# The row copy of each tile's softmax sums is held in the zone of nine buffers, not in the zone of four

## The chip, the cores and the metric

The kernel runs on one core of a Trainium2 chip. The metric is the device time of one execution in microseconds; smaller is better. A core has five engines that run their own instruction streams in order: TensorE (PE in the profile; its weight loads are listed as PEld), VectorE (DVE), ScalarE (ACT), GpSimd (POOL) and the sync engine, whose stream here only issues DMA transfers (SPq). They wait for each other through semaphores. Data lies in on-chip memory, in accumulators that TensorE writes (banks), and in the chip's main memory.

## The reference

One step of a model with two layers on 1024 latent tokens and 256 context tokens, 1024 channels wide. Layer 0 projects the normalised and modulated input to queries, keys, values and gates of two attention mixers: A attends to all keys, B to a window of 128 tokens on each side, with a learned extra logit ("sink") in the softmax; both see all context keys. The outputs are multiplied by SiLU gates and projected back. Layer 1 mixes with a Fourier transform over positions and channels, gated, and projected. A final normalisation follows.

What matters for this change is the softmax's denominator. Cut to the lines that compute it:

```python
def softmax_sink(sc, sink):
    sink = sink.astype(jnp.float32)
    m = jnp.maximum(jnp.max(sc, axis=-1, keepdims=True), sink)
    p = jnp.exp(sc - m)
    return p / (jnp.sum(p, axis=-1, keepdims=True) + jnp.exp(sink - m))
...
return jnp.concatenate([oa * jax.nn.silu(ga), ob * jax.nn.silu(gb)], axis=-1) @ w_out
```

The kernel doesn't divide the probabilities. It sums them, takes reciprocals once for each tile of 128 tokens and all 16 heads, and multiplies these into the gate before the output projection.

## The kernel before, in words

**Tiles and units.** The 1280 tokens are ten tiles `t` of 128 rows (0 to 7 latent, 8 and 9 context). Attention runs in units `(t, g, pr)`: `g` = 0, 1 are the two key/value heads of mixer A, 2 and 3 those of mixer B, and `pr` a pair of heads. A unit has two halves. `soft` (lines 941 to 1018) computes scores on TensorE, running minima on VectorE (lines 967, 1011) and the exponential on ScalarE (line 974), which also leaves the sum of each head in `SU`. `weigh` (line 1040) transposes the probabilities on TensorE (line 1050), splits them into a high and a low part (ScalarE through the helper at line 277, VectorE at line 1053), and multiplies them with the values (line 1056). Then ScalarE copies the lower half of the accumulator into a buffer `lo_sb` (line 1065), VectorE adds it to the upper half in a buffer `os_` (line 1067), and a store of `os_` to `od` in main memory is kept in `held` until the next unit (line 1073).

`attend` walks through the units of mixer A, then those of mixer B in the order 0 2 3 4 7 6 5 1 8 9 of the tiles; in mixer B `weigh` runs two units behind `soft`. Between the units a `Filler` puts in other work: gates (`gate0`: a tanh buffer `th` at line 822, the gate `gs` at line 826, stored to `gd` at lines 838 to 844), loads and splits of the output weights (`out_weights`, load at line 1112, splits in lines 277 and 283), folding of a weight for layer 1 (`fold_piece`), and output projections of tiles that are complete (`proj_in`, `proj_step`, `out_proj`).

**The row copy.** When the last unit of a tile in mixer B is done, `after` calls `totals(t)`. It adds the sink terms, sums, takes reciprocals on VectorE (lines 1023 to 1029), transposes the 128 x 16 result to 16 x 128 on TensorE (line 1032), copies it from the accumulator into a buffer `row` on ScalarE (line 1035) and stores it to `scd` in main memory (line 1037: one or two pieces, as the tiles are stored in another order of tokens). `proj_in` reads `scd` back, spread over the partitions (line 1225), and GpSimd multiplies it with the gate and that with `od` (lines 1226 and 1227).

**Zones.** On-chip buffers lie in zones. `ZONES` gives the number of buffers and their width in words of 4 bytes: "h" has 9 of 512 words (2 KB in each partition), "e" has 4 of 256 words (1 KB).

```python
ZONES = {"u": (26, 1032), "w": (8, 1032), "q": (2, 1024), "pt": (3, 1024), "p": (4, 1280), "h": (9, 512), "e": (4, 256)}
```

`take(tag, shape)` takes the buffer of a zone that was dropped longest ago, and `drop` puts one at the end of the zone's queue. Both happen when the program is written down, in the order of the code, so which buffer follows which is fixed and doesn't depend on times. An instruction that writes a taken buffer waits until all users of the buffer's earlier content are done: readers on an engine, or a store that must have landed.

In this stretch "e" serves `lo_sb`, `os_` and, before the change, `row`. "h" serves `th` and `gs` of the gates, the raw halves of weight rows before they are split (line 1112), pieces of the fold, and scratch of the projections (`yt` in lines 1247 and 1347).

**Order.** The order of the instructions on each engine is not that of the code. The program is made with `schedule_with_timeline_sim=True`: a planner goes through all instructions with due times of its own model, and lets each engine issue what is ready first, with the dependences through the buffers as given. So when the buffer of an instruction changes, its dependences change, and the planned order can change from there on. On the chip each engine then follows this fixed order, and one that waits holds up all that stands behind it. Only for the first phase is the order on the sync engine written out by hand; it ends before the stretch that the change touches.

Of the kernel before, what the change touches and what calls it, by code (L numbers as in the profile page):

```python
# [17 lines left out]
P = 128  # L18
# [121 lines left out]
def hybrid_step(ctx: ExitStack, tc: tile.TileContext, I, O):  # L140
# [15 lines left out]
    def take(tag, shape, dt=F32):  # L156
        tags = (tag,) if isinstance(tag, str) else tag
        z = min((t for t in tags if spare[t]), key=lambda t: spare[t][0])
        i = spare[z].popleft()[1]
        size = 2 if dt == BF16 else 4  # L160
        for s in shape[1:]:
            size *= s
        assert size <= 4 * ZONES[z][1]
        made[0] += 1
        return Buf(z, i, up.tile(list(shape), dt, tag=f"{z}{i}", name=f"{z}{made[0]}", bufs=1))

    def drop(*bufs):
        for b in bufs:
            stamp[0] += 1
            spare[b.zone].append((stamp[0], b.idx))  # L170
# [5 lines left out]
    def t_bank(name, dt=F32):  # L176
        return bank("t", name, dt)
# [843 lines left out]
    def totals(t):  # L1021
        tot = sm.tile([P, 16], F32, tag="tot", name=f"tot{t}", bufs=2)
        dve.tensor_add(tot[:, 0:8], NM[:, t], sink)  # L1023
        act.activation(SU[:, t, 8:16, 1], tot[:, 0:8], AF.Exp)
        dve.tensor_reduce(out=tot, in_=SU[:, t], op=ALU.add, axis=AX.X)
        dve.tensor_scalar(tot, tot, 2.0, None, op0=ALU.mult)
        dve.reciprocal(tot, tot)
        byp = sm.tile([P, 16], F32, tag="byp", name=f"byp{t}", bufs=2)
        dve.tensor_copy(byp.rearrange("p (h c) -> p h c", h=2), tot.rearrange("p (c h) -> p h c", h=2))  # L1029
        tot = byp  # L1030
        tp = t_bank(f"tt{t}")
        pe.transpose(tp[0:16, 0:P], tot, ident)
        row = take("e", (16, P))
        rev = t in (2, 3, 6, 7, 9)
        act.activation(row[..., ::-1] if rev else row.a, tp[0:16, 0:P], AF.Copy)
        for r, c0, b0, n in PIECES[t]:
            sp.dma_start(scd[r, :, :, c0 : c0 + n].rearrange("h c n -> (h c) n"), row[:, b0 : b0 + n])
        drop(row)
# [158 lines left out]
    def after(un):  # L1197
        t, g, pr = un
        if g > 1:
            clock[0] += 1  # L1200
        if g < 2 and un == lastA[g]:
            swap_kv(g)
        if un == last_g2:
            drop(*kvb[2])
        if g == 3 and pr == 1:
            totals(t)
            finished[t] = clock[0]
# [772 lines left out]
```

## Time and profile before

| | |
|---|---|
| median of 3 runs | 1191.29 us (1189.96 to 1192.39) |
| the profiled execution's own time | 1188.89 us |
| its span, first to last instruction | 1187.1 us |
| TensorE busy, share of the span | 1150.7 us, 97% |
| VectorE, ScalarE, GpSimd busy | 835.5, 569.4, 329.3 us |
| mean granted TensorE clock | 0.998 |
| row copies (line 1035) | 10, first at 596.7 us, last at 803.0 us |
| stores of rows (line 1037) | 16, first at 599.4 us |

How to read it: times are microseconds from the start of the span. In a list of groups or a timeline a line gives start, duration, engine, line of the kernel, operation, what is written and read (buffer numbers left out, and a zone's name stands for its buffers), and in brackets how long the engine stood idle before it and what ended that. In a table by stretches there stand for each engine its busy time and its number of instructions, then the granted clock as a share of full speed, the share in which the DMA engines were busy, and GB/s. The chain of waits is followed back from the last instruction, at each step to what released it.

### The profile page before, as it was taken

What the parts mean: (1) busy time and instruction counts of PE and PEld (TensorE: products, weight loads), DVE (VectorE), ACT (ScalarE), POOL (GpSimd) and SP (SyncE); (2) the same over time, 40 slices, a digit from 0 to 9 for tenths busy, and PEclk for the clock granted to TensorE, in tenths of its full rate; (3) what the DMA queues carried; (4) which work ended last, traced back from release to release, by engine and by line L of the source; (5) the groups of instructions that cost most, each with busy time, mean ns of one, the idle gap of its engine ahead of it and who ended that gap; (6) DMA issues with size and microseconds to landing.
All of it is one profiled execution on the core that took longest, in us unless ns stands there. A gap on an engine that the chain in (4) does not pass through costs nothing.

```text
span 1187.1 us, 22024 instructions
## 1 busy us (share of the span) xinstructions
PE 1150.7 (97%) x8103; PEld 1032.0 (87%) x8103; DVE 835.5 (70%) x1994; ACT 569.4 (48%) x1149; POOL 329.3 (28%) x294
## 2 busy tenths in 40 slices
PE   8999999999999999999999989999999999999997
PEld 6788899999999999899989887887877888998886
DVE  2489788877777776668888977876765962378543
ACT  4442455556656555556666674522363234342211
POOL 2355645512222221010110045275331226100001
PEclk9999999999999999999999999999999999999999
DMA  9978512323523232344352586785213426264321
GB/s 330 374 252 265 172 44 67 103 78 105 161 72 96 77 96 76 87 126 123 86 153 75 149 233 201 226 256 160 89 45 129 165 93 189 95 205 152 125 107 54
DMA packets 130096, 168.81 MB, mean 142 GB/s; under 512 B 26298, under 2 KB 86454, under 8 KB 129988
## 3 DMA queue, kind: packets, MB, share of 16 engines
q1 hardware_dynamic: 127476, 158.74, 43.4%
q0 software_dynamic: 2368, 8.39, 2.4%
q8 instruction: 64, 1.05, 0.4%
q14 instruction: 44, 0.36, 0.1%
q10 hardware_dynamic: 144, 0.26, 0.1%
HBM read 123.19 MB, written 44.16 MB: 141 GB/s over the span
## 4 chain that ended last, share of the span: by engine, by line
PE 76%; DMA 10%; DVE 6%; ACT 3%; issue 2%; SPq 2%; POOL 1%; POOLq 0%; DVEq 0%; ACTq 0%
PE of L265 9%; PE av L1056 9%; PE ga L265 8%; PE pt L1050 8%; PE q L265 8%; PE sL L933 5%; PE oz L265 4%; PE u L265 4%; PE g1O L265 4%; PE g1E L265 3%; PE kv L265 3%; PE sC L933 3%; PE g1c L265 2%; DMA od<-e 2%; DMA q<-qd 2%
## 5 line engine op out<-in xcount | busy, mean ns | idle before, releaser
L277 ACT ACTIVATE pt<-pt 128x512 fp32r<-128x512 f32 (+1 forms) x265 | 147.0, 576 | 107.6 <-PE pt L1050 60.3
L1053 DVE TENSOR_TENSOR pt<-pt,pt 128x512 fp32r<-128x512 f32 (+1 forms) x264 | 170.8, 658 | 37.9 <-ACT pt L277 37.0
L1056 PE MATMUL av<-pt,u 128*128 128x256 f32 x1008 | 167.0, 289 | 3.0 <-DVE e L1067 2.0
L1050 PE MATMUL pt<-identr,p 128*128 128x128 f32 x1008 | 156.9, 272 | 1.2 <-ACT p L974 0.8
L1056 PEld LDWEIGHTS av<-pt,u 128*128 128x128 f32 x1008 | 138.4, 189 | 7.1 <-DVE e L1067 2.6
L265 PE MATMUL q<-w,u 128*128 128x256 f32 x960 | 143.8, 287 | 0.0
L265 PEld LDWEIGHTS q<-w,u 128*128 128x128 f32 x960 | 126.9, 189 | 4.9 <-issue 0.8
L1050 PEld LDWEIGHTS pt<-identr,p 128*128 128x128 f32 x1008 | 119.3, 140 | 7.9 <-ACT p L974 1.0
L974 ACT ACTIVATE p<-p,nm 128x1280 f32<-128x1280 f32 (+1 forms) x80 | 95.5, 1194 | 62.3 <-DVE p L967 62.1
L265 PE MATMUL ga<-u,w 128*128 128x512 f32 (+1 forms) x576 | 124.4, 360 | 0.8 <-DVE byp L1029 0.5
L265 PEld LDWEIGHTS ga<-u,w 128*128 128x128 f32 x576 | 93.8, 188 | 15.0 <-ACT pt L277 1.2
L283 POOL TENSOR_TENSOR w<-h,w 128x512 fp32r<-128x512 f32 x38 | 51.1, 1363 | 143.5 <-DVE w L279 116.7
L933 PE MATMUL sL<-u,q 128*128 128x512 f32 x256 | 82.5, 411 | 1.4 <-DMA q<-qd 1.4
L974 ACT ACTIVATE p<-p,NM 128x640 f32<-128x640 f32 (+2 forms) x80 | 59.1, 739 | 38.1 <-DVE p L967 38.0
L933 PE MATMUL sC<-u,q 128*128 128x256 f32 x320 | 61.5, 293 | 2.3 <-DMA q<-qd 2.0
L967 DVE TENSOR_SCALAR_CACHE_REDUCE p<-sL 128x512 f32<-128x512 f32 x64 | 43.9, 685 | 23.5 <-PE sL L933 14.6
L967 DVE TENSOR_SCALAR_CACHE_REDUCE p<-sL,nm 128x512 f32<-128x512 f32 x64 | 47.7, 745 | 13.5 <-PE sL L933 12.6
L265 PE MATMUL oz<-u,w 128*128 128x512 f32 x192 | 56.9, 400 | 0.0
L707 POOL TENSOR_TENSOR h<-h,rope 128x512 f32<-128x512 f32 (+1 forms) x18 | 21.9, 1217 | 125.8 <-ACT h L790 80.0
L933 PEld LDWEIGHTS sC<-u,q 128*128 128x128 f32 x320 | 48.8, 189 | 6.4 <-DVE tot L1023 1.7
L265 PE MATMUL oz<-u,u 128*128 128x512 f32 x160 | 47.8, 402 | 4.3 <-DVE h L1248 2.4
L283 POOL TENSOR_TENSOR u<-h,u 128x512 fp32r<-128x512 f32 x16 | 21.1, 1325 | 108.6 <-ACT u L277 104.3
(728 smaller groups left out, 2590.1 us busy)
## 6 DMA issues: line engine op xcount, KB each, us to landing
q<-qd SPq DMA_DIRECT2D x80, 256.0 KB
h<-i_w_in SPq DMA_DIRECT2D x40, 256.0 KB
p<-i_ada_w SPq DMA_DIRECT2D x18, 512.0 KB
h<-i_w_out SPq DMA_DIRECT2D x32, 256.0 KB
pt<-i_ada_w SPq DMA_DIRECT2D x15, 512.0 KB
qd<-pt SPq DMA_DIRECT2D x20, 256.0 KB
q<-i_ada_w SPq DMA_DIRECT2D x9, 512.0 KB
qd<-q SPq DMA_DIRECT2D x18, 256.0 KB
```

The source lines that it names most:

```text
L265: pe.matmul(out, a, b, start=i == 0, stop=i == n - 1)
L277: act.activation(out, in_, AF.Copy)
L283: pick("lo" + lc, lc).tensor_sub(dst_l, src, dst_h)
L707: pick("rope", XE["rope"]).tensor_mul(t1.rearrange("p t h (b c) -> p t (h b) c", b=2), y.rearrange("p t h (b c) -> p t (h b) c", b=2), cb)
L933: pe.matmul(ps, q_at(q, s, hc), keys, start=s == 0, stop=s == 1)
L967: dve.tensor_scalar(p[i][:, end[i] : end[i] + n], ps, sign, last[i], op0=ALU.mult, op1=ALU.min, accum_out=c)
L974: act.activation(p[i][:, 0 : end[i]], p[i][:, 0 : end[i]], AF.Exp, bias=last[i], scale=-1.0, accum_out=SU[:, t, hd + i, 0:1],)
L1050: pe.transpose(tp[:, jj * 256 + i * P : jj * 256 + i * P + P], p[i][:, off : off + P], ident)
L1053: dve.tensor_sub(pt[:, 1, 0:n], tp[:, 0:n], pt[:, 0, 0:n])
L1056: pe.matmul(acc, vv, pt[:, s, jj * 256 : jj * 256 + 256], start=c + jj + s == 0, stop=c + jj == nt - 1 and s == 1,)
```

## The change

The buffer for `row` is taken from zone "h" instead of zone "e". Shape, type and instructions stay the same; so do the ten copies and the sixteen stores. What differs is which earlier content the copy waits for, and which later content waits for the row's store, in both zones: each take behind the first row gets another buffer of the cycle than before.

```diff
         tot = byp
         tp = t_bank(f"tt{t}")
         pe.transpose(tp[0:16, 0:P], tot, ident)
-        row = take("e", (16, P))
+        row = take("h", (16, P))
         rev = t in (2, 3, 6, 7, 9)
         act.activation(row[..., ::-1] if rev else row.a, tp[0:16, 0:P], AF.Copy)
         for r, c0, b0, n in PIECES[t]:
```

## The prediction

> **What bounds the kernel now.** I read first the page: span, busy shares, shares of the chain.
>
> ```profile
> span 1187.1 us, 22024 instructions
> PE 1150.7 (97%) x8103; PEld 1032.0 (87%) x8103; DVE 835.5 (70%) x1994; ACT 569.4 (48%) x1149; POOL 329.3 (28%) x294
> PE 76%; DMA 10%; DVE 6%; ACT 3%; issue 2%; SPq 2%; POOL 1%; POOLq 0%; DVEq 0%; ACTq 0%
> ```
>
> TensorE is busy for 1150.7 of 1187.1 us. The change neither adds nor removes a TensorE instruction, so it can only move the 36.4 us in which TensorE stands idle, or the clock. The profiled execution took 1188.89 us, 1.8 us more than its span; the median of the three runs, 1191.29 us, lies 2.4 us above it. I make the sum against 1188.89 and add 2.4 us at the end.
>
> The ten row copies run from 596.7 to 803.0 us (the next fence but one). So I read the busy times of that stretch next.
>
> ```profile
> core 0: us, PE busy (x) PEld busy (x) DVE busy (x) ACT busy (x) POOL busy (x), PEclk, DMA share, GB/s
> 600.00:690.00 90.00, 86.14 (x577) 77.84 (x576) 75.45 (x233) 59.51 (x137) 9.11 (x7) 1.00 0.48 127
> 690.00:740.00 50.00, 45.97 (x282) 40.87 (x282) 37.32 (x93) 28.44 (x65) 26.45 (x26) 1.00 0.80 233
> 740.00:815.00 75.00, 71.28 (x374) 59.82 (x372) 62.62 (x116) 29.01 (x71) 37.70 (x20) 0.98 0.71 217
> ```
>
> TensorE is idle for 90 - 86.14 = 3.86 us, then 4.03 us, then 3.72 us: 11.6 us in all. Everything before 596.7 us stays as it is, and what comes later can only shift.
>
> **The wait that the change removes.** The row copy is line 1035 on ScalarE. Its own view gives one long wait.
>
> ```profile
> L1035 ACT ACTIVATE e<-tt x10: 250/259/270, 596.7 to 803.0; 16x128 f32<-16x128 f32 x10
>   DMA od<-e: 5.0, 1
> ```
>
> I followed the takes and drops of zone "e" through the code. One unit of attention takes two buffers, lo_sb and os_, and a row takes one more, so each row turns the cycle of four by one place. Nine rows get a buffer that last held a lo_sb, which only VectorE reads. The tenth row (tile 9, the last) gets the buffer of the os_ of unit (8, 3, 1), whose store had just been issued. The timelines of that place, ScalarE, VectorE, TensorE, GpSimd and the DMA queue in turn:
>
> ```profile
> 796.79 1.16 ACT L1361 ACTIVATE p<-u,r11y 128x1024 f32<-128x1024 f32 x1 [4.67 <-POOL r11y L244]
> 802.99 0.27 ACT L1035 ACTIVATE e<-tt 16x128 f32<-16x128 f32 x1 [5.04 <-DMA od<-e]
> 803.28 0.38 ACT L1065 ACTIVATE e<-av 64x256 f32<-64x256 f32 x1
> ```
> ```profile
> 801.53 0.69 DVE L1249 TENSOR_TENSOR pt<-pt,h 128x512 f32<-128x512 f32 x1 [4.12 <-DMA pt<-i_xp]
> 802.14 1.28 DVE L1362 SCALAR_TENSOR_TENSOR pt<-w,r11y,p 128x1024 f32<-128x1024 f32 x1
> 803.69 0.42 DVE L1067 TENSOR_TENSOR e<-av,e 64x256 f32<-64x256 f32 x1 [0.27 <-ACT e L1065]
> 804.03 2.69 DVE L283 TENSOR_TENSOR u<-u,w 128x1024 fp32r<-128x1024 f32 x1
> ```
> ```profile
> 804.16 0.74 PE L1056 MATMUL av<-pt,u 128*128 128x256 f32 x4 [0.97 <-DVE e L1067]
> 806.77 0.79 PE L265 MATMUL oz<-u,u 128*128 128x512 f32 x1 [1.87 <-DVE u L283]
> ```
> ```profile
> 799.19 1.04 POOL L279 CAST w<-u 128x1024 fp32r<-128x1024 f32 x1
> 808.28 0.31 POOL L1524 MEMSET e<- 128x256 f32 x1 [2.65 <-DMA od<-e]
> ```
> ```profile
> 796.91 0.62 SPq L1073 DMA_DIRECT2D od<-e  x1
> ```
>
> In "h" the tenth row takes the buffer of a yt of the second projected tile. VectorE read the first tile's results from 718.77 us and that yt at 741.14, some 60 us earlier:
>
> ```profile
> 718.77 0.69 DVE L1248 TENSOR_TENSOR h<-oz,u 128x512 f32<-128x512 f32 x1 [4.27 <-PE oz L265]
> ...
> 741.14 0.69 DVE L1249 TENSOR_TENSOR u<-u,h 128x512 f32<-128x512 f32 x1
> ```
>
> So it can start when ScalarE ends line 1361, at 797.95 us: 5.04 us of ScalarE wait go. Queued behind it on ScalarE is line 1065 (lo_sb of the next unit); the SP queue holds the row's store, and behind it a weight load, stores of os_ and the loads of the sums for the last tiles. For the end only one of them counts: line 1065 releases line 1067 on VectorE, and this and line 283 release the two waits of TensorE (0.97 and 1.87 us). But VectorE has its own cover: it waits 4.12 us for the residual rows and is busy with lines 1249 and 1362 until 803.42. Line 1067 waited only 0.27 us for ScalarE after that. **Term 1: -0.27 us**, and everything behind it on VectorE moves by the same. If the cover were gone (lines 1067 and 283 planned ahead of 1249), it would be worth more; that is a rival below.
>
> **The rest of "e".** Without rows the four buffers fall into two pairs: lo_sb always follows a lo_sb two units back, os_ an os_. One other wait on this zone stands in the trace:
>
> ```profile
> 725.86 0.42 DVE L1067 TENSOR_TENSOR e<-av,e 64x256 f32<-64x256 f32 x1 [3.92 <-DMA od<-e]
> ```
>
> This os_ of unit (6, 3, 0) follows the os_ of unit (8, 2, 0), two units earlier, with rows or without, so the 3.92 us stay. The memset at 808.28 gets a buffer whose store was issued at 796.91, not after 804 us, and loses its 2.65 us, but GpSimd only casts and multiplies for later tiles there: no gain. **Term 2: 0**, bounds 0 and -0.3 us (as term 1).
>
> **Zone "h".** Ten takes more on nine buffers. This moves every take of "h" behind the first row, and what matters is which earlier user a DMA into "h" now has to wait for. Following the cycle: the loads of the output weights (line 1112) of the first three half rows come behind later users than before, above all the third behind the row of tile 2, whose store was issued at 627 us; before it followed a gate piece. The fifth comes earlier.
>
> ```profile
> 627.01 1.00 SPq L1037 DMA_DIRECT2D scd<-e  x2
> 655.10 0.36 SPq L1112 DMA_DIRECT2D h<-i_w_out  x1
> ```
>
> Of these early loads nothing is needed before the first projection, whose first result is read at 718.77 (above), some 90 us on, so I cost them at nothing: their cover is this distance. The price, if a load is placed so that ScalarE waits for it, is read from the worst place of that kind, in the chain of waits:
>
> ```profile
> 668.97 0.50 SPq L838
> 669.56 3.75 DMA h<-i_w_out
> 673.33 0.64 ACT u L277
> ...
> 675.76 3.37 DMA gd<-h
> 679.19 5.40 DMA h<-i_w_out
> ```
> ```profile
> 684.61 0.63 ACT L277 ACTIVATE u<-h 128x512 fp32r<-128x512 f32 x1 [3.85 <-DMA h<-i_w_out]
> ```
>
> Here "h" itself sets the pace: a gate piece is stored, the next load waits for the buffer, ScalarE waits for the load, and the next gate piece waits behind ScalarE. Now the load at 669.56 (it followed the tanh buffer of the gate piece, free at 669.5) follows the stored half of the same piece, whose store was issued at 668.97. With the 3.37 us of such a store it starts at 672.4, 2.8 us later. The load ahead of it, which left at 655.10, comes to 669.5. Bounds: nothing, where the planner puts other ScalarE work ahead; 2.8 us of TensorE where all is handed on. To choose, I take how much of such waits reached TensorE in this stage. The view of line 1112, 590 to 690 us, gives what ScalarE waited:
>
> ```profile
>   ACT u L277: 13.2, 8
> ```
>
> TensorE was idle for 3.86 us in 600 to 690, at most 3.86 / 13.2 = 0.29 of it. **Term 3: 2.8 x 0.29 = +0.8 us**, nearer to the lower bound.
>
> **The row as an earlier user of "h".** A row holds its buffer until its store has landed. The store that the chain shows took 2.12 us:
>
> ```profile
> 734.75 2.12 DMA scd<-e
> ```
> ```profile
> 682.06 1.12 SPq L1037 DMA_DIRECT2D scd<-e  x2
> ```
> ```profile
> 687.73 0.38 ACT L822 ACTIVATE h<-ga 128x256 f32<-128x256 f32 x1
> ```
>
> The row of tile 4 is followed by the tanh of a gate piece, at 687.73: 683.2 + 2.1 = 685.3, so there are 2.4 us to spare. The other nine are followed well over 10 us later, except for the third weight load above. **Term 4: 0**, bounds 0 and +2.1 us.
>
> **Sum**: -0.27 + 0 + 0.8 + 0 = +0.5 us: 1189.4 us for an execution like the profiled one, 1191.8 us as a median. What a measurement of this kernel tells from no change is about 0.2%, 2.4 us. My forecast: no measurable difference.
>
> **Rivals.**
>
> *Slower: zone "h" hands its delay on.* The place is 668 to 690 us. From the point where ScalarE reaches the split of the late load with nothing else ready, TensorE loses the full 2.8 us in one gap. What such a gap does beside the idle time is seen at 803 us:
>
> ```profile
> 803.00:807.00 4.00, 1.16 (x6) 0.76 (x6) 3.73 (x4) 1.02 (x3) 2.63 (x1) 0.94 0.27 83
> 807.00:810.00 3.00, 3.00 (x8) 2.33 (x9) 3.00 (x4) 0.00 (x0) 1.67 (x2) 0.52 0.63 176
> ```
>
> After 2.84 us without work (in two gaps) the granted clock was 0.52 for 3 us: 3 x 0.48 = 1.4 us more. So +2.8 + 1.4 = +4.2 us, 1195.5 us. For it: ScalarE already waited 3.85 us there. Against: at 690 to 740 us the DMA share is 0.80 and TensorE waits for transfers anyway, which can take up a delay.
>
> [...]
>
> *Faster: the stall at 803 us goes.* The order on each engine is planned anew from the first row on. With the row no longer waiting for a store, the planner may put lines 1067 and 283 ahead of line 1249: line 1065 could end at 798.6 us, the cast at 799.19 is done at 800.23, and line 283 with its 2.69 us would end at 802.9, before TensorE runs dry at 803.2. Gain 2.84 + 1.4 = 4.2 us: 1187.1 us. For it: VectorE stands idle 4.12 us there. Against: TensorE and DMA rows around it do not depend on the row, so the planner has no reason of its own to turn the two round.
>
> *The wait is only moved.* If the tenth row found its buffer in "h" late, ScalarE would wait again and the 0.27 us stay; 1192.1 us, inside the forecast. The cycle speaks against it.
>
> **How the numbers follow.** No measurable difference 0.36 (the moved wait, 0.05, is in it), slower 0.32, faster 0.32: the two cases have equal prices, and since every engine's order is planned again over 200 us with 11.6 us of TensorE idle time in it, a result of either sign is nearly as likely as none. Both signs hold most of the chance, so: the likeliest case alone covers 1189.4 to 1194.2 us. The range takes in the bounds: below, the faster case and the 3.86 us idle time of 600 to 690, 1191.3 - 4.2 - 3.9 = 1183.2; above, the slower case and one more load of 3.75 us handed on whole, 1191.3 + 4.2 + 3.8 = 1199.3.
>
> **What would show it.** Term 1: line 1035 has no wait on a store in the view of its line, and line 1067 at the place of 803 us begins without its 0.27 us while TensorE still waits there for line 283. Term 2: VectorE's wait of about 3.9 us near 726 us is still there. Term 3: ScalarE's wait on the weight loads, 590 to 690 us, grows from 13.2 us by 2 to 3 us, and TensorE's idle time there from 3.9 to some 4.7 us. Term 4: nobody waits for the row's store on account of "h". I am wrong if TensorE's idle time of 600 to 690 changes by more than 2 us, if the gap at 803 us goes, or if a wait appears behind 815 us.

## The result and the profile after

The changed kernel takes 1200.72 us (median of 6 runs, 1198.90 to 1203.05), the kernel before 1190.45 us (6 runs, 1187.80 to 1192.39). The ratio is 1.0090 with a 95% interval of 1.0077 to 1.0102: slower by 0.9%, some 10 us (the two medians differ by 10.3 us). That is 1.4 us above the upper end of the predicted range, 1199.3 us. The profiled execution after took 1200.05 us.

The page of the changed kernel: span, busy shares, shares of the chain.

```profile
span 1198.3 us, 22021 instructions
PE 1156.0 (96%) x8103; PEld 1036.7 (87%) x8103; DVE 838.0 (70%) x1994; ACT 570.3 (48%) x1149; POOL 330.4 (28%) x294
PE 77%; DVE 9%; DMA 8%; ACT 2%; issue 2%; SPq 1%; POOL 1%; POOLq 0%; DVEq 0%; ACTq 0%
```

TensorE has the same 8103 matmuls. Its idle time grew from 36.4 to 1198.3 - 1156.0 = 42.3 us and its busy time by 5.3 us. Of the busy time, some changes without any change of the kernel: a repeat of the kernel before (again, below) has 1153.7 us busy in a span of 1189.6 us, so 3.0 us more, and 35.9 us idle. VectorE's share of the chain rose from 6 to 9%.

The table by stretches (busy us and instructions of TensorE, its weight loads, VectorE, ScalarE, GpSimd; granted clock, DMA share, GB/s) of the changed kernel, and then the last stretch of the kernel before, which the prediction did not show:

```profile
600.00:690.00 90.00, 86.00 (x561) 76.68 (x559) 71.71 (x222) 55.85 (x126) 8.17 (x7) 1.00 0.45 127
690.00:740.00 50.00, 43.27 (x268) 39.23 (x269) 36.49 (x100) 29.73 (x72) 22.75 (x22) 0.97 0.70 207
740.00:815.00 75.00, 73.02 (x394) 61.98 (x393) 57.60 (x119) 31.59 (x74) 38.40 (x24) 1.00 0.75 231
815.00:900.00 85.00, 79.46 (x376) 64.49 (x374) 63.01 (x85) 35.36 (x67) 32.91 (x23) 0.98 0.26 91
```
```profile
815.00:900.00 85.00, 83.95 (x402) 67.98 (x401) 59.03 (x100) 40.72 (x80) 29.43 (x23) 1.00 0.31 103
```

TensorE's idle time went from 3.86 to 4.00 us in 600 to 690, from 4.03 to 6.73 in 690 to 740, from 3.72 to 1.98 in 740 to 815, and from 1.05 to 5.54 behind 815 us.

The wait that the change was to remove is gone. The view of the row copy's line (its form; what its engine waited for; who waited for it):

```profile
L1035 ACT ACTIVATE h<-tt x10: 248/258/268, 596.5 to 797.4; 16x128 f32<-16x128 f32 x10
  PE tt L1032: 7.2, 5
  PE pt L1050: 0.7, 2
```

No store stands there any more. Instead ScalarE waits 7.2 us in five places for the transpose: the copies now stand earlier in ScalarE's order, which is one sign that the planner has laid the work out anew.

The longest waits of TensorE, from its timeline:

```profile
644.08 0.86 PE L1056 MATMUL av<-pt,u 128*128 128x256 f32 x5 [1.09 <-DVE e L1067]
710.52 0.48 PE L933 MATMUL sC<-u,q 128*128 128x256 f32 x2 [2.03 <-DMA q<-qd]
718.68 0.47 PE L933 MATMUL sC<-u,q 128*128 128x256 f32 x2 [3.40 <-DMA q<-qd]
822.77 1.22 PE L265 MATMUL oz<-u,w 128*128 128x512 f32 x2 [4.81 <-DVE e L1067]
```

Two places are new: queries that come late at 708 to 719 us (the expectations below say 703 to 718 us), and a wait of 4.81 us for line 1067 at 818 to 823 us. The gap of before at 803 to 807 us is gone.

To see what each place costs I compared the start of the k-th matmul of TensorE in the two traces. Up to the 4700th (587 us), where the orders of all engines are still the same, the profiled execution after is already 3.63 us behind: the start of the program takes longer or shorter from one execution to the next (in again it is 2.29 us longer). Without that, the changed kernel is 7.5 us behind at the end. This table of shifts in us against the trace of before is from one execution each; a repeat of the kernel before (again) and before_less, which has the same order on all engines but GpSimd, show how far one stretch moves by itself: up to 2.6 us, so single entries below that say little. The edges are the matmuls 4700, 5350, 5600, 6000 and 6500. The shift tells when the k-th matmul starts; in another order that can be a matmul of another size.

```
stretch (us in before)    587-689  689-733  733-814  814-918  rest    sum
again (= before)            -1.0     +0.5     +1.0     -0.6   +0.2   +0.2
after                       +1.3     +2.9     -3.8     +6.0   +1.1   +7.5
own                         +0.4     -1.9     -4.3     +6.8   -0.2   +0.8
turn_h                      +1.9     +2.6     +1.9     +5.6   +2.5  +14.4
h_turn_e                    +4.0     +3.1     -3.6     +6.7   +1.4  +11.7
h_first                     +1.4     +3.8     +1.2     +6.1   +0.3  +12.8
h_late                      +1.3     +0.3     -0.3     +1.6   -0.1   +2.7
h_last                      +0.1     +0.3     +0.7      0.0   +0.2   +1.2
turn_once                   -1.0     +1.0     -4.1     +3.1   +0.7   -0.2
rows_2                      -0.5     +4.3     +1.7     -0.4   +1.6   +6.6
rows_3                      +1.6     -1.2     -3.7     +2.9   +0.2   -0.1
rows_4                      +1.8     -0.6     -4.7     +2.9   +0.2   -0.3
h_scalar                    +4.1     +4.7     -1.4     +6.2   +0.5  +14.2
h_less                      +1.8     +2.0     -1.3     +1.0   +0.4   +4.0
own_less                    +1.3     -2.3     -2.2     +1.2   +0.1   -1.8
before_less                 -0.3     -2.6     -2.6     +0.1   +0.4   -5.0
before_dve                  +1.1     -1.2     -1.5     -0.6   +1.0   -1.2
```

**The first place.** The chain of waits of the changed kernel, at the points that the chain of before does not have in this form:

```profile
633.02 4.83 DMA h<-i_w_out
637.88 0.64 ACT u L277
...
639.90 2.62 DMA h<-i_w_out
...
688.35 4.42 DMA scd<-h
...
698.71 11.67 DMA q<-qd
...
714.44 4.11 DMA q<-qd
```

Two early weight loads (line 1112) stand in the chain: ScalarE waits for them before it goes on with the attention (2.84 and 2.64 us, ahead of line 277 at 637.88 and 642.55 us), although nobody needs the weights yet. At 688.35 us the store of a row in "h" stands in it. Then come two query loads; the first took 11.67 us (9.42 us in the chain of before), the second was issued late. The sync engine's timeline around it:

```profile
706.65 1.41 SPq L1037 DMA_DIRECT2D scd<-h  x2
710.45 1.90 SPq L1073 DMA_DIRECT2D od<-e  x2
713.31 0.39 SPq L554 DMA_DIRECT2D wd<-h  x1
713.79 1.25 SPq L938 DMA_DIRECT2D q<-qd  x2
```

The same queue in the kernel before:

```profile
706.52 1.25 SPq L938 DMA_DIRECT2D q<-qd  x2
...
712.28 0.59 SPq L938 DMA_DIRECT2D q<-qd  x1
```

There a query load leaves at 706.52 us, here at 713.79 us; 3.63 us of this are the later start. A row's store, two stores of `os_` and a store of the fold stand ahead of it here, and the queue does not run through them: by the list of its waits from 700 to 714 us it waits 7.4 us for earlier transfers to land (a store of `os_` 2.7, the first query loads 3.1, gate stores 1.6); ahead of the load at 706.52 us before it waits 2.2 us for that. So the second load is late at least in part because the transfers before it were slow. While the first load was under way the DMA engines were busy 0.97 of the time, and 1.02 of it in the 9.42 us before.

**The second place.** VectorE, ahead of TensorE's wait at 822.77, and GpSimd at the same time:

```profile
812.19 0.67 DVE L1248 TENSOR_TENSOR h<-oz,u 128x512 f32<-128x512 f32 x1
812.79 2.50 DVE L1363 SCALAR_TENSOR_TENSOR p<-w,r11y,p 128x1024 f32<-128x1024 f32 x1
815.21 1.21 DVE L1378 TENSOR_TENSOR p<-w,pt 128x1024 f32<-128x1024 f32 x1
816.35 2.86 DVE L1249 TENSOR_TENSOR pt<-pt,h 128x512 f32<-128x512 f32 x1
819.13 2.05 DVE L1379 TENSOR_TENSOR pt<-w,pt 128x1024 f32<-128x1024 f32 x1
```
```profile
811.55 2.66 POOL L1226 TENSOR_TENSOR u<-u,u 128x1024 f32<-128x1024 f32 x1 [2.07 <-DMA u<-gd]
815.53 3.13 POOL L1226 TENSOR_TENSOR q<-q,u 128x1024 f32<-128x1024 f32 x1 [1.33 <-issue]
818.61 1.50 POOL L279 CAST u<-p 128x1024 fp32r<-128x1024 f32 x1
```

Line 1249 took 2.86 us where the median of its form is 0.69, and it ended 819.21 - 818.66 = 0.55 us behind GpSimd's multiplication. Lines 1363 and 1379 end 1.08 and 1.07 us behind GpSimd's instructions, which is close to the 1.27 and 1.21 us that they take in the kernel before (at 806.64 and 810.95 us): they look as if they began when GpSimd had ended. Line 1248, which reads one accumulator and one buffer, ran beside GpSimd in its usual 0.67 us. What line 1249 took beyond its median, 2.86 - 0.69 = 2.17 us, is close to the 818.66 - 816.35 = 2.31 us that GpSimd still had to run when it began. So I took the long instructions for VectorE held up while GpSimd runs; how the one holds up the other, these rows do not show.

### The profile page after: what moved, and what is told of

The parts are those of the page before. It is cut to its first block, busy times and chain, and to the rows that moved or that the text cites. A ratio compares the mean times of both kernels' runs of the same rounds, so it can differ in the third digit from the quotient of the medians.

```text
span 1198.3 us, 22021 instructions
## 1 busy us (share of the span) xinstructions
PE 1156.0 (96%) x8103; PEld 1036.7 (87%) x8103; DVE 838.0 (70%) x1994; ACT 570.3 (48%) x1149; POOL 330.4 (28%) x294
## 3 DMA queue, kind: packets, MB, share of 16 engines
q8 instruction: 64, 1.05, 0.4%
## 4 chain that ended last, share of the span: by engine, by line
PE 77%; DVE 9%; DMA 8%; ACT 2%; issue 2%; SPq 1%; POOL 1%; POOLq 0%; DVEq 0%; ACTq 0%
PE of L265 9%; PE av L1056 8%; PE q L265 8%; PE pt L1050 8%; PE ga L265 7%; PE oz L265 6%; PE sL L933 5%; PE u L265 4%; PE g1E L265 4%; PE g1O L265 4%; PE kv L265 3%; PE sC L933 3%; PE g1c L265 2%; DMA q<-qd 2%; DMA h<-i_w_out 1%
## 5 line engine op out<-in xcount | busy, mean ns | idle before, releaser
L265 PEld LDWEIGHTS oz<-u,w 128*128 128x128 f32 x192 | 36.5, 192 | 14.0 <-DVE e L1067 5.0
```

What stands on the lines that cost most here:

```text
L265: pe.matmul(out, a, b, start=i == 0, stop=i == n - 1)
```

## The experiments

All ratios are against the kernel before, run on the same chip beside them, with their 95% interval. My first theory after the result was the turned cycle of "h"; its rivals were the freed row (nothing waits at 803 us any more, and the order changes for that), and the cycle of "e".

**again**: the kernel before once more.

> The kernel before once more, as a control. Median within 0.2% of the runs of before. The start of the program is the same in both kernels, but in the two profiled executions the first 110 us took 3.7 us longer after the change than before it. If this is spread between executions, the profile of this control may show any offset between 0 and 4 us there; if it comes with the change, it shows 0 to 1 us.

0.9987 (0.9969 to 1.0006). No difference.

**own**: the row leaves "e", but "h" stays as it was.

```diff
-ZONES = {"u": (26, 1032), "w": (8, 1032), "q": (2, 1024), "pt": (3, 1024), "p": (4, 1280), "h": (9, 512), "e": (4, 256)}
+ZONES = {"u": (26, 1032), "w": (8, 1032), "q": (2, 1024), "pt": (3, 1024), "p": (4, 1280), "h": (9, 512), "e": (4, 256), "r": (1, 128)}
...
-        row = take("e", (16, P))
+        row = take("r", (16, P))
```

> The row copy gets a zone of its own with one buffer, so zone h keeps its cycle, zone e loses its rows as in the change, and the copy waits only for the row before it. If the loss comes from the turned cycle of zone h: as fast as before, 1188 to 1193 us. If it comes from the row copy being free to start early, so that ScalarE and the sync engine issue it ahead of other work: as slow as after, 1196 to 1203 us, with ScalarE waiting some 7 us for the transposes of the rows.

1.0039 (1.0020 to 1.0057). So a part of the loss is there without any turn of "h". The gap at 803 us is gone here too, and a wait of 4.24 us near 812 to 816 us has taken its place.

**turn_h**: the row stays in "e"; behind each row a buffer of "h" is taken and dropped unused.

```diff
         drop(row)
+        drop(take("h", (16, P)))
```

> The row copy stays in zone e; at each row a buffer of zone h is taken and dropped unused, so only the cycle of zone h turns as in the change. If the turned cycle is the cause: as slow as after, 1196 to 1203 us, with the order of the weight loads as after. If the free row copy is the cause: as before, 1188 to 1193 us.

1.0107 (1.0074 to 1.0140): a loss of the same size, with no row in "h" at all. So a loss like this does not need a row that holds a buffer of "h" until its store has landed. That it is the same loss is not shown: the order is not that of the changed kernel, and besides the late queries TensorE has a long wait near 765 us that the changed kernel does not have (line 1054 here is line 1053 of before):

```profile
PE sC L933 <- DVE pt L1054: 6.1, 1, 6.1
```

**h_turn_e**: the change, and "e" turned as before.

```diff
-        row = take("e", (16, P))
+        row = take("h", (16, P))
...
         drop(row)
+        drop(take("e", (16, P)))
```

> The change, and a buffer of zone e taken and dropped unused at each row, so that lo_sb and os_ follow each other in zone e as before the change. If the new cycle of zone e is part of the loss, it is faster than after by over 3 us; if it has no part, it stays at 1199 to 1203 us.

1.0111 (1.0089 to 1.0133). The order of all engines but GpSimd is that of the changed kernel; the cycle of "e" has no part that shows.

**Which rows.** h_first has the rows of the tiles 0, 2, 3, 4, 7 in "h", h_late the other five, h_last only that of tile 9, whose wait the change removes; turn_once turns "h" by one buffer behind the row of tile 4.

```diff
-        row = take("e", (16, P))
+        row = take("h" if t in (0, 2, 3, 4, 7) else "e", (16, P))  # h_first
+        row = take("h" if t in (6, 5, 1, 8, 9) else "e", (16, P))  # h_late
+        row = take("h" if t == 9 else "e", (16, P))  # h_last
```
```diff
         drop(row)
+        if t == 4:
+            drop(take("h", (16, P)))  # turn_once
```

> The rows of tiles 0, 2, 3, 4, 7 lie in zone h, those of tiles 6, 5, 1, 8, 9 in zone e as before. Theory A (the loss comes from the early rows: they put weight loads and gate pieces of zone h behind later users, and every engine's planned order changes from there on; VectorE's planned order here is that of the changed kernel, ScalarE's and the sync engine's differ from it in a few places): 1.007 to 1.010 times before, with TensorE's waits for query loads at 703 to 718 us and its wait of some 4.8 us near 817 to 823 us both there. Theory B (part of the loss comes from the late rows, the wait near 817 us above all): 1.003 to 1.006, without that wait.

> The rows of tiles 6, 5, 1, 8, 9 lie in zone h, those of tiles 0, 2, 3, 4, 7 in zone e as before. The planned order of VectorE and GpSimd is then the one of before, and TensorE's, ScalarE's and the sync engine's differ from it in a few places. Theory A (loss from the early rows alone): 0.998 to 1.001; ScalarE's wait of 5.04 us at 803 us is gone, TensorE's gap there stays within 0.3 us of 2.84 us, since VectorE still waits for the residual rows first. Theory B (the late rows cost): 1.003 to 1.006, with the wait near 817 us.

> Only the row of tile 9, the one whose wait the change was to remove, lies in zone h; ScalarE's order differs from before by this row moving one place ahead, every other order is that of before. This measures the first term of the prediction by itself: -0.27 us, ratio 0.998 to 1.001; ScalarE's wait of 5.04 us at 803 us gone and TensorE's gap there 0 to 0.3 us shorter. If the row's wait had carried the gap at 803 us: -4.2 us, 0.9965.

> Rows stay in zone e; one buffer of zone h is taken and dropped unused, once, behind the row of tile 4, so that every later take of h gets the next buffer of the cycle. No instruction is added. Theory A, as a matter of which load waits for which user at 668 to 690 us: part of the loss, 1.003 to 1.008, with TensorE waiting for query loads at 703 to 718 us. If the loss needs the rows as users of h or all the early turns: 0.998 to 1.002.

h_first 1.0099 (1.0072 to 1.0127), h_late 0.9986 (0.9969 to 1.0003), h_last 0.9995 (0.9978 to 1.0012), turn_once 1.0005 (0.9990 to 1.0019). The early rows bring the whole loss, the late ones none. Both new waits are in h_first:

```profile
717.69 0.77 PE L933 MATMUL sC<-u,q 128*128 128x256 f32 x2 [4.37 <-DMA q<-qd]
826.63 1.22 PE L265 MATMUL oz<-u,w 128*128 128x512 f32 x2 [4.80 <-DVE e L1067]
```

In h_last ScalarE's 5.04 us are gone, its row is copied at 795.1 us, and TensorE's two waits at the old place are not shorter (1.69 and 2.23 us against 0.97 and 1.87; in again 1.26 and 1.83, so part of this comes by itself):

```profile
L1035 ACT ACTIVATE h<-tt x1: 266/266/266, 795.1 to 795.1; 16x128 f32<-16x128 f32 x1
```
```profile
807.86 0.74 PE L1056 MATMUL av<-pt,u 128*128 128x256 f32 x4 [1.69 <-DVE e L1067]
810.83 0.72 PE L265 MATMUL oz<-u,u 128*128 128x512 f32 x1 [2.23 <-DVE u L283]
```

**How many early rows.** rows_2, rows_3 and rows_4 have the rows of the first two, three, four tiles of the order in "h".

```diff
-        row = take("e", (16, P))
+        row = take("h" if t in (0, 2) else "e", (16, P))  # rows_2
+        row = take("h" if t in (0, 2, 3) else "e", (16, P))  # rows_3
+        row = take("h" if t in (0, 2, 3, 4) else "e", (16, P))  # rows_4
```

> The rows of tiles 0 and 2 lie in zone h, the other eight in zone e. Theory A1 (the loss comes from particular buffers: a load of an output weight that falls behind the row of tile 2 and delays what ScalarE does behind its split): 1.003 to 1.006, with weight loads in the chain of waits at 630 to 650 us and the same late query loads at 703 to 718 us. Theory A2 (each turn gives another planned order, and what that costs does not grow with the number of rows in h): anything from 0.997 to 1.010, and the times of this run and the two with three and four rows do not rise in order; the late query loads appear in some and not in others.

> The rows of tiles 0, 2 and 3 lie in zone h. Theory A1: above the run with two rows by 0 to 0.003, never below it. Theory A2: no order between them, 0.997 to 1.010.

> The rows of tiles 0, 2, 3 and 4 lie in zone h; the row of tile 4 is now one of those whose store a gate's tanh waits for near 690 us. Theory A1: 1.007 to 1.010, nearly the whole loss. Theory A2: no order between them, 0.997 to 1.010.

1.0109 (1.0066 to 1.0153), 1.0039 (1.0018 to 1.0061), 1.0042 (1.0021 to 1.0063): two rows cost more than three or four, and five cost as much as two. Theory A1, a loss that grows with the buffers that are turned, has fallen. The pattern is that of A2, each turn another planned order at its own price, though rows_2 lies a little above the 1.010 named for it. The single executions of rows_4 spread from 1190.63 to 1198.75 us; the table of shifts has the shortest execution of rows_2, of rows_3 and of rows_4, so their rows look better than their medians.

The late queries go with the loss. TensorE's wait for query loads between 590 and 1000 us is 5.3 to 8.0 us in all six complete kernels that lost 0.9% or more (the changed kernel, turn_h, h_turn_e, h_first, rows_2, and h_scalar below), and 1.3 to 4.4 us in all other complete ones, with 4.1 us in turn_once, which lost nothing measurable. This is an agreement between runs, not a run that takes the wait alone away.

rows_4 also serves as a control for the second place. Lines 1363, 1379 and 1249 take their plain time on VectorE there, while GpSimd waits for a load:

```profile
808.51 1.27 DVE L1363 SCALAR_TENSOR_TENSOR p<-w,r11y,p 128x1024 f32<-128x1024 f32 x1
811.44 1.21 DVE L1379 TENSOR_TENSOR pt<-w,pt 128x1024 f32<-128x1024 f32 x1
812.57 0.68 DVE L1249 TENSOR_TENSOR pt<-pt,h 128x512 f32<-128x512 f32 x1
```
```profile
813.75 2.89 POOL L1226 TENSOR_TENSOR u<-u,u 128x1024 f32<-128x1024 f32 x1 [11.81 <-DMA u<-gd]
```

**h_scalar**: the change, with the rows' stores on another queue.

```diff
-            sp.dma_start(scd[r, :, :, c0 : c0 + n].rearrange("h c n -> (h c) n"), row[:, b0 : b0 + n])
+            act.dma_start(scd[r, :, :, c0 : c0 + n].rearrange("h c n -> (h c) n"), row[:, b0 : b0 + n])
```

> The change, with the rows' stores issued from ScalarE's own DMA queue behind the copy instead of the sync engine's queue. If the query loads of 703 to 718 us come late because they stand behind the row's store and the stores of os_ on the sync engine: the wait of TensorE for them there falls from 5.9 us to 1 to 2 us, and the ratio to 1.002 to 1.006. If they come late because the DMA engines are full: the wait stays at 4 to 6 us and the ratio at 1.007 to 1.011.

1.0121 (1.0088 to 1.0154). TensorE's wait for queries stayed:

```profile
PE sC L933 <- DMA q<-qd: 5.3, 2, 4.0
```

With no row's store on the sync engine, its next query load still left at 714.19 us. So the row's store ahead of it is not what makes it late. The wait is the one expected for full DMA engines (4 to 6 us), the ratio a little above the 1.007 to 1.011 named for it, and the orders of the engines changed as well, so that this is not shown. Here the queue issues nothing from 704.99 to 711.05 us, for 6.1 us ahead of that load.

**h_less, before_less, own_less**: line 1226 left out for the tiles 8 and 9, in the changed kernel, in the kernel before and in own; the order of TensorE, VectorE, ScalarE and the sync engine stays that of each kernel.

```diff
-            pick("pm", XE["pm"]).tensor_mul(gl.a, gl.a, rl.a)
+            if r < 8:
+                pick("pm", XE["pm"]).tensor_mul(gl.a, gl.a, rl.a)
```

> The change, with the multiplication of gates and sums (line 1226, on GpSimd) left out for tiles 8 and 9, so their outputs lack the softmax denominators. TensorE, VectorE, ScalarE and the sync engine keep the order of the changed kernel. Theory C (the wait near 817 to 823 us is VectorE held up by GpSimd: 1.23 + 2.17 + 0.84 = 4.24 us of stretched instructions): the wait falls from 4.81 us to 0.6 to 1.5 us, and the ratio to before from 1.009 to 1.004 to 1.006. Theory D (the order of VectorE alone makes it): the wait stays over 3.5 us and the ratio at 1.008 to 1.011.

> The kernel before with the same two multiplications left out (tiles 8 and 9 lack the softmax denominators); every other engine keeps the order of before. Theory C: line 283 at 804 us takes 1.2 to 1.9 us instead of 2.69, the wait of TensorE for it falls from 1.87 us to some 0.5 us: ratio 0.997 to 1.000. Theory D: 0.999 to 1.001.

> Rows in a zone of their own (one buffer), and the same two multiplications left out for tiles 8 and 9; every other engine keeps the order of that kernel. Theory C: its wait near 812 to 816 us falls from 4.24 us to 0.5 to 1.5 us, the ratio from 1.004 to 0.999 to 1.002. Theory D: 1.003 to 1.006.

h_less 1.0061 (1.0045 to 1.0077), before_less 0.9986 (0.9968 to 1.0004), own_less 0.9992 (0.9974 to 1.0009). The timelines of VectorE and of TensorE in h_less, whose line numbers behind 1226 are higher by one:

```profile
814.73 1.26 DVE L1364 SCALAR_TENSOR_TENSOR p<-w,r11y,p 128x1024 f32<-128x1024 f32 x1
817.06 0.67 DVE L1250 TENSOR_TENSOR pt<-pt,h 128x512 f32<-128x512 f32 x1
817.66 1.21 DVE L1380 TENSOR_TENSOR pt<-w,pt 128x1024 f32<-128x1024 f32 x1
```
```profile
821.44 0.73 PE L265 MATMUL oz<-u,w 128*128 128x512 f32 x2 [1.32 <-DVE e L1067]
```

With the same order, the three instructions have their plain times and TensorE's wait fell from 4.81 to 1.32 us. In own_less it fell from 4.24 to 1.50 us. Theory C is shown: the second wait has most of its length from VectorE held up by GpSimd (3.49 of 4.81 us here, 2.74 of 4.24 us in own_less). What it is worth against before is another matter. The kernel before has such a place of its own, at 803 us: line 283 took 2.69 us there beside this multiplication, and 1.20 us in before_less. As quotients of the ratios, own without these instructions is 0.9992 / 0.9986 = 1.0006 times before without them, the changed kernel 1.0061 / 0.9986 = 1.0075. Each quotient is uncertain by some 0.25%. As far as that tells, the collision accounts for own's loss, and for little of the changed kernel's 1.0090.

**before_dve**: the kernel before, complete, with line 1226 on VectorE for the tiles 8 and 9.

```diff
-            pick("pm", XE["pm"]).tensor_mul(gl.a, gl.a, rl.a)
+            (dve if r >= 8 else pick("pm", XE["pm"])).tensor_mul(gl.a, gl.a, rl.a)
```

> The kernel before, complete, with the multiplications of tiles 8 and 9 on VectorE instead of GpSimd (1.2 us each there). VectorE has some 2.4 us more to do between 790 and 820 us, where it waits for transfers, and GpSimd no longer holds it up. Theory C: 0.996 to 1.001; if VectorE's added work falls on the path of the last projections: 1.001 to 1.003. Planned orders change in a few dozen places.

1.0002 (0.9983 to 1.0022): nothing gained. No version beat the kernel before by more than its interval.

## Why the prediction was wrong

I had forecast no measurable difference, 1191.8 us, from 1183.2 to 1199.3.

**Term 1** (-0.27 us) is too small to be measured, and nothing speaks against it: the row alone, in h_last, is worth a ratio of 0.9995 with 0.17% to either side. VectorE's cover did hold, since ScalarE's 5.04 us went and TensorE gained nothing.

**Term 2** (zone "e": 0). Its price was right: h_turn_e has the time of the change, within the intervals. What was to show it did not come: the wait of 3.92 us near 726 us was to stay, and between 590 and 830 us VectorE, in its new order, waits only 0.6 us for stores of `os_`.

**Term 3** (+0.8 us for 600 to 690 us). ScalarE's wait for the weight loads grew from 13.2 us to this:

```profile
ACT u L277 <- DMA h<-i_w_out: 16.9, 9, 4.0
```

That is 3.7 us more, where 2 to 3 were expected. TensorE's idle time in 600 to 690 us grew by 0.14 us, and its shift over this stretch is +1.3 us, which is no more than the stretch moves by itself; so the size of the term is not contradicted, but its place was wrong. At 668 to 690 us next to nothing was lost. TensorE stands idle for 2.60 us in 620 to 650 us, where it had no idle time before, and the chain leads from there to the early weight loads that I had costed at nothing because "their cover is this distance" of 90 us to their use. The two splits that waited for their loads held up the attention behind them in ScalarE's order (the exponential of line 974 came at 638.42 us, the copy of line 1065 at 643.20 us), however late their own results were needed. Against this, TensorE stands idle for 1.61 us at 662 to 672 us in the kernel before, and not in the changed kernel.

**Term 4** (0). The chain puts the store of tile 4's row, at 688.35 us, ahead of the gate's tanh, so the 2.4 us to spare were used up: the store took 4.42 us, where I had reckoned with 2.12. Still nobody on the path of TensorE stood idle for it: ScalarE had other instructions to do until that tanh, and the store is not among ScalarE's waits from 685 to 700 us. So the price of 0 held.

**The step that failed** is the one ahead of the terms: "what comes later can only shift". With it, all four terms were worked out in the order of the kernel before, and nothing behind 815 us was looked at. The prediction did say, in its rivals, that the order is planned anew from the first row on, but it brought this in as two cases of equal price and chance and not as a term. What comes later does not only shift. In the two traces I compared the order of the instructions of TensorE and of VectorE (line, operation and names, without buffer numbers) with that of before, and counted those out of place. In h_last it is none, in h_late 2 and none, and both cost nothing measurable. In the changed kernel it is 271 and 144, in own 147 and 93, in turn_h 209 and 119, in rows_2, rows_3 and rows_4 219 to 255 and 128 to 137, in turn_once 131 and 89. The ratios of these new orders lie between 1.000 and 1.011 and follow neither the number of rows in "h" nor these counts.

The new order of the changed kernel is where its loss stands: +2.9 us at 689 to 733 us (5.4 us by 730 us at the late queries, of which 2.5 us come back at a wait that the kernel before has at 733 us), -3.8 us at 733 to 814 (the gap at 803 us goes), +6.0 us at 814 to 918 (the wait at 818 to 823 us, and a clock of 0.52 in the 3 us behind it) and +1.1 us after that. No term of the sum has these sizes. The gap that goes and the wait that comes cancel but for 2.2 us, so the largest single piece left is that of the late queries; h_turn_e and h_first, whose orders are nearly those of the changed kernel, have +3.1 and +3.8 us there. The "slower" rival had the wrong place and less than half the price; the "faster" rival's gap did go, at about the price named for it (3.8 against 4.2 us), and another of the same kind opened 15 us later. Two of my own signs of error came true: the gap at 803 us went, and a wait appeared behind 815 us.

**What stays open**: which change of order makes the queries late. Each kernel that moved something there was planned anew, so no run takes away that cause alone. No run holds the old order with the new buffers either. So that the order, and not the waits on other buffers by themselves, carries the loss is argued: from h_late, which moves five rows, keeps the order but for a few places and costs nothing, and from the ratios that do not follow the rows.

## What to carry to other kernels

Where a planner orders the engines from the dependences, a change of a buffer has, as I read these runs, two prices: the waits it moves, which can be read from the profile, and a new order behind it, which can't. Of the eight new orders measured here without other changes to the work (the changed kernel's, own, turn_h, turn_once, h_first, and rows_2 to rows_4) seven lost and none won. Compare the planned orders of the two versions first: where they differ in a handful of places, as in h_late, the sum of the waits held, and where they differ in a hundred or more, it need not (it was off by 0.4 to 1.1% in seven kernels, and held in turn_once). When an instruction of VectorE takes two or four times its usual time (here 2.69 us instead of 1.20, and 2.86 us instead of 0.69), look at what GpSimd does at that moment, before the time is put down to a wait.

## What the runs showed of the hardware

Line 1249 on VectorE took 2.86 us while GpSimd multiplied, instead of 0.69, and that multiplication, which began 0.32 us behind line 1378 on VectorE, took 3.13 us, where line 1226 takes 2.40 at 790.90 us before. I had used such a number, the 2.69 us of line 283, as a plain duration. The rows of the kernel before show GpSimd beside it:

```profile
802.84 2.79 POOL L1226 TENSOR_TENSOR u<-u,u 128x1024 f32<-128x1024 f32 x1 [2.61 <-DMA u<-gd]
```

In own the granted clock was lower behind its wait of 4.24 us. In 817 to 823 us, the table by stretches of own and of own_less:

```profile
817.00:823.00 6.00, 6.00 (x17) 4.68 (x17) 2.25 (x2) 1.06 (x1) 0.47 (x1) 0.56 0.62 198
```
```profile
817.00:823.00 6.00, 6.00 (x28) 4.88 (x27) 3.18 (x5) 1.57 (x2) 0.00 (x0) 1.00 0.73 239
```

Behind 4.24 us of waiting the clock was 0.56, and behind 1.50 us 1.00: TensorE shows 6.00 us busy in both, with 17 matmuls in the one and 28 in the other. The first 587 us, the same work in all these kernels, differ between the profiled executions by up to 3.8 us (0.10 to 3.79 us behind the one of before, at the 4700th matmul), which is more than most of the terms argued about here.
